# Attention with unnormalised exponentials: reciprocal row sums carried through DRAM to the output projection

## The chip, the cores and the metric

The kernel runs on one core of a Trainium2 chip, in one launch. The metric is the device time of that launch in microseconds (us), the median of several runs. The core has five engines that work through queues of their own: TensorE (PE in the profile, with its weight loads as PEld), VectorE (DVE), ScalarE (ACT), GpSimd (POOL) and SyncE (SP), which in this kernel issues most of the DMA transfers. Each engine takes its instructions strictly in the order of its queue, and waits on semaphores for the others.

## What is computed

One trunk layer over 1280 tokens: 1024 latent tokens and 256 context tokens, D_MODEL = 1024. Everything is float32. Of the layer, this concerns the attention and the projection behind it:

```
def one_block(qi):
    s = jnp.einsum('bqkgd,bskd->bkgqs', qi, kf) * scale
    p = jax.nn.softmax(s, axis=-1)
    return jnp.einsum('bkgqs,bskd->bqkgd', p, vf)
...
o_a = block_attention(q, k_all, v_all)
o_h, s_final = hgrn_branch(...)
g = jax.nn.sigmoid(gl.astype(F32)).reshape(b, l, N_BRANCH, D_MODEL)
merged = g[:, :, 0] * (o_h @ w_ho) + g[:, :, 1] * (o_a @ w_ao)
return merged @ w_out, k, v, s_final
```

There are 8 query heads of 64 channels on 2 key/value heads. A latent token attends to 512 cached keys and all 1024 latent keys; a context token attends to the 256 context keys. `o_h` is the output of a second branch, a gated linear recurrence (the HGRN branch, 4 heads of 128 channels). Behind the mixer stand a residual, a second norm and an MLP of width 4096.

## The kernel before

**Tiles and stages.** The tokens are cut into three token tiles `TT`: t = 0 and t = 1 with 512 latent tokens each, t = 2 with the 256 context tokens. Products in full precision are made of three TensorE products: every operand is split into a rounded high part `hi` (ACT, line 277) and a rest `lo` (DVE, line 278), and `hi*hi`, `hi*lo` and `lo*hi` are added in PSUM (lines 308 to 310 and 325 to 327). The program runs in this order: input norm and the first projections; attention, into which the projections of the HGRN branch are interleaved; the HGRN recurrence, into which the projections of the branch gates GL are interleaved; the output projection of both branches; the rest of the layer with the MLP.

**One unit of attention.** `Unit` (line 661) stands for one head, one token tile and 256 query rows (`q2` counts these within the tile, `j` is 0 or 1 for the two blocks of 128 rows). For t < 2 the keys come in three groups of 512 (`i` = 0, 1, 2), so a unit has six tasks (j, i); for t = 2 there is one group of 256 keys and a unit has two tasks. There are 32 long units and 8 short ones. The steps of a task are:

- `score` (line 686): PE makes the scores in PSUM (`ps_s`, line 697), DVE takes their row maximum (`mx`, line 698) and, when the block's groups are all there, the negated overall maximum (`ngm`, line 702).
- `expo` (line 705): ACT makes the exponentials in SBUF (`pexp`, line 708) and at the same time their row sums (`sm`). After the block's last group DVE adds the sums of the groups (`rs`, line 711) and takes the reciprocal (line 712).
- `norm` (line 714): each tile of exponentials is multiplied with the reciprocal `rs` of its row, in place. `NORM = [g_, v]` hands these products in turn to POOL and to DVE (line 716).
- `trans` (line 733): PE turns 256 keys by 256 queries of the weighted exponentials (`ps_t`, line 738); ACT and DVE split them into `pTh` (line 741) and `pTl` (line 742).
- `value` (line 745): PE multiplies the values `Vl` with `pTh` (line 753) and with `pTl` (line 754), and adds over all keys. At the unit's end ACT and DVE bring the two halves of the result together (`pvt`, line 762, and `oa`, line 763). When the second head of a pair has done its last rows of the token tile, the pair's outputs, 128 channels by n tokens, go to DRAM as `OA` (line 766).

**What sets the order.** `events` (line 718) lists a unit's steps with a place in time each, counted in transposes of 256 keys; `attention` (line 791) sorts the events of all units, and in front of each lets `Filler` issue its share of the interleaved projections. That fixes the order of PE's queue, which is scheduled by hand. The queues of DVE, ACT, POOL and SP are put in order by the framework, from the same program and a model of the durations. Small tiles such as `mx`, `sm` and (after the change) `rs` come from rings: `T(4)` has 8 buffers of 4 columns each, which are used again in turn, each once its last reader is done; where that reader is a DMA, the next writer waits for the DMA.

**The interleaved projections.** Their weights come as `wraw` (1 MB per DMA, two buffers, line 282) and are split by ACT and DVE into `wsp` (128 x 1024 per instruction, lines 277 and 278).

**The output projection.** Lines 1141 to 1149 load, for t in the order 0, 2, 1, the eight tiles of 128 channels by n tokens, four of the HGRN branch (`OH`) and four of attention (`OA`), into tiles `or`, and split each into two `hs` tiles. The `hs` tiles are the buffers in which the normed input `hT` of the layer has stood until then, so a split waits until the last product of the GL projection with that buffer is done. The `or` tiles come from a ring of 20 buffers in SBUF (ring "X"). From line 1165 on PE multiplies them with the two branches' weights, DVE gates the results (line 1182).

Of the kernel before, what the change touches and what calls it, by code (L numbers as in the profile page):

```python
# [12 lines left out]
ALU = mybir.AluOpType  # L13
AX = mybir.AxisListType

P = 128
# [9 lines left out]
TT = [(0, 512, 0), (512, 512, 0), (1024, 256, 1)]  # L26
# [18 lines left out]
def build(ctx, tc, I, O, C):  # L45
    nc = tc.nc
    v, s_, g_, pe, sp = nc.vector, nc.scalar, nc.gpsimd, nc.tensor, nc.sync
# [42 lines left out]
    def H(t, dt=F32R, name="hs"):  # L90

        return hp.tile([P, 512] if t < 2 else [P, 2, 256], dt, tag="h%d" % t, name=name, bufs=16 if t < 2 else 8)

    def T(n, name="tiny"):
        return tp.tile([P, n], F32, tag="tiny%d" % n, name=name, bufs=8 if n <= 16 else 2)

    def DR(shape, name, dt=F32):
        return dp.tile(list(shape), dt, name=name)

    def dma(out, in_):  # L100
        sp.dma_start(out=f32(out), in_=f32(in_))
# [4 lines left out]
    def f32(ap):  # L106
        return ap.bitcast(F32)
# [105 lines left out]
    def hpair(t):  # L213
        n = TT[t][1]
        if n == 512:
            return H(t), H(t)
        x = h_first.pop() if h_first else H(2)
        return x[:, 0, :], x[:, 1, :]
# [57 lines left out]
    def split(hi, lo, raw):  # L276
        s_.activation(hi, raw, AF.Copy)  # L277
        return v.tensor_tensor(lo, raw, f32(hi), op=ALU.subtract)  # L278
# [104 lines left out]
    KG = [512, 512, 512, 256]  # L383
# [205 lines left out]
    for idx in range(len(steps)):  # L589
        while idx >= KC - 1 and done <= min(idx + AHEAD, len(steps) - 1):  # L590
            t, kc = steps[done]
# [7 lines left out]
        t, kc = steps[idx]  # L599
# [58 lines left out]
    OA = [[DR((P, n), "OA%d_%d" % (c, t)) for t, (_, n, _) in enumerate(TT)] for c in range(4)]  # L658
    OH = [[DR((P, n), "OH%d_%d" % (c, t)) for t, (_, n, _) in enumerate(TT)] for c in range(4)]

    class Unit:


# [22 lines left out]
        def score(self, j, i):  # L686
            nk = len(self.kts)
            if (j, i) == (0, 0):
                self.qh = q_at[self.h, self.t]
                self.ps, self.mx, self.sm, self.rs = {}, {}, {}, {}  # L690
            if i == 0:
                self.mx[j], self.sm[j] = T(4, "mx"), T(4, "sm")
            n = KG[self.kts[i]]
            q0 = self.q2 * 256 + j * P
            pq = PS("s")
            for var in range(2):
                pe.matmul(pq[:, 0:n], self.qh[:, q0:q0 + P], K[self.g][var][self.kts[i]], start=(var == 0), stop=(var == 1))  # L697
            v.tensor_reduce(self.mx[j][:, i:i + 1], pq[:, 0:n], axis=AX.X, op=ALU.max)  # L698
            self.ps[j, i] = pq
            if i == nk - 1:  # L700
                ngm = T(1, "ngm")
                v.tensor_reduce(ngm, self.mx[j][:, 0:nk], axis=AX.X, op=ALU.max, negate=True)  # L702
                self.mx[j] = ngm

        def expo(self, j, i):
            n, nk = KG[self.kts[i]], len(self.kts)
            e = self.Ps[j][i] = S(name="pexp")
            s_.activation(e[:, 0:n], self.ps.pop((j, i))[:, 0:n], AF.Exp, bias=self.mx[j], accum_out=self.sm[j][:, i:i + 1])  # L708
            if i == nk - 1:
                rs = self.rs[j] = T(1, "rs")  # L710
                v.tensor_reduce(rs, self.sm[j][:, 0:nk], axis=AX.X, op=ALU.add)
                v.reciprocal(rs, rs)

        def norm(self, j, i):
            x = self.Ps[j][i][:, 0:KG[self.kts[i]]]
            NORM[(i + j) % len(NORM)].tensor_scalar(x, x, self.rs[j], None, op0=ALU.mult)  # L716

        def events(self, s0):
            if self.nstep == 1:
                ev = [(-4, 0, 0), (-3.5, 1, 0)]  # L720
                out = [(a, self.score, (j, i)) for a, j, i in ev]
                out += [(a + 1, self.expo, (j, i)) for a, j, i in ev]
                out += [(a + 2, self.norm, (j, i)) for a, j, i in ev]
            else:
                out = [(a, self.score, (j, i)) for (j, i), a in zip(self.tasks, (-7, -6.9, -6, -4, -3.9, -3))]
                out += [(a, self.expo, (j, i)) for (j, i), a in zip(self.tasks, (-5.4, -4.9, -4.4, -2.4, -1.9, -1.4))]
                out += [(a, self.norm, (j, i)) for (j, i), a in zip(self.tasks, (-4.35, -3.45, -2.45, -1.35, 0.1, 2.1))]
            for p2 in range(self.nstep):
                out.append((p2, self.trans, (p2,)))
                out.append((p2 + ((2.5, 2.3, 2.0, 1.7, 1.5, 1.3)[p2] if self.nstep > 1 else 1.5), self.value, (p2,)))  # L730
            return [(s0 + a, f, x) for a, f, x in out]
# [33 lines left out]
            if self.h % 2 == 1 and self.q2 == n // 256 - 1:  # L765
                dma(OA[self.h // 2][self.t], o_at[self.h // 2, self.t][:, 0:n])

    NORM = [g_, v]
    gone, keyed, copied = [None], [None], [None]
    q_at, o_at = {}, {}  # L770
    K = [[[None] * 4 for _ in range(2)] for _ in range(2)]
    V = [[None] * 4 for _ in range(2)]

# [17 lines left out]
    def attention(fill):  # L791
        units = []
        for ts_ in ((0, 1), (2,)):
            for h0 in (4, 6, 0, 2):
                for t in ts_:
                    for hh in range(2):
                        for q2 in range(TT[t][1] // 256):
                            units.append(Unit(h0 // 4, h0 + hh, t, q2, [0, 1, 2] if t < 2 else [3],
                                              q2 == 0 and (t < 2 or hh == 0), hh == 0 and q2 == 0))
        events, s0 = [], 0  # L800
        for u in units:
            if u.new_q:
# [340 lines left out]
    for t in MT:  # L1143
        n = TT[t][1]
        for c in range(8):
            r = S(name="or")
            dma(r[:, 0:n], (OH if c < 4 else OA)[c % 4][t])
            oT[t][c] = hpair(t)
            split(oT[t][c][0], oT[t][c][1], r[:, 0:n])
    mg = [[None] * KC for _ in range(3)]  # L1150
# [14 lines left out]
    for c2 in range(4):  # L1165
        r = wp.tile([P, 8, 256], F32, tag="wraw", name="wraw", bufs=2)
        for i, nm in enumerate(("w_hgrn_out", "w_attn_out")):
            dma(r[:, 4 * i:4 * i + 4, :], I[nm][:, c2 * 256:(c2 + 1) * 256].rearrange("(k p) c -> p k c", p=P))
        for half in range(2):
# [4 lines left out]
            for t in MT:  # L1174
                n = TT[t][1]
# [108 lines left out]
    for b, half in turns:  # L1284
        t, off = b // 4, (b % 4) * P
# [62 lines left out]
    def raw1(i):  # L1348
        return wraw(I["w_ff1"], KC, i * 256)
# [30 lines left out]
    for i in range(NP):  # L1380
        r = raw1(i)
        for half in range(2):
            j = 2 * i + half
# [5 lines left out]
            if half == 0:  # L1389

                x = pw.tile([P, 4, P], F32, tag="at", name="at", bufs=4)
# [43 lines left out]
    ev = pool("ev", "right")  # L1435
    W2 = I["w_ff2"]
    op0 = []
# [221 lines left out]
    def fw_tile(name):  # L1659
        return xo.tile([P, D], F32, tag="fw", name=name, bufs=1)  # L1660
# [80 lines left out]
    x = fw_tile("y34")  # L1741
# [85 lines left out]
```

## Time and profile before

| | |
|---|---|
| median of 3 runs | 2055.07 us (2054.92 to 2057.83) |
| the profiled execution, its own time | 2055.24 us |
| span of its instructions | 2053.1 us, at a mean granted TensorE clock of 0.998 |
| attention, by the first and last split of transposed exponentials | 171.8 to 706.8 us |
| DVE busy from 153 to 714 us | 394.18 of 561.00 us |
| POOL busy from 153 to 714 us | 181.68 of 561.00 us |
| DMA from 153 to 714 us | 0.24 of the engines' time, 78 GB/s |
| splits of `or` tiles (DVE) | 24, from 1024.4 to 1039.7 us |

The profile names a group of instructions by the line that records it, the engine, the operation and the tiles, as `out<-in`. A time "idle before" is how long the engine had nothing to do just before an instruction; behind `<-` stands what released it. In a timeline each row gives the start, the time that the row's instructions cover, and in brackets the idle time before it. Matmuls are pipelined: the next one starts before the one before it has ended, so that two starts lie closer together than one matmul lasts.

### The profile page before, as it was taken

Reading aid. Unit: us, or ns where it says so; the run is one execution under the profiler, and the core shown is the slowest. Engines: PE = TensorE matmul, PEld = TensorE weight load, DVE = VectorE, ACT = ScalarE, POOL = GpSimd, SP = SyncE. Lnnn points to the kernel's source line nnn. Section 1 sums busy time; section 2 is a strip of 40 time slices with the busy share of each in tenths; the row PEclk is TensorE's granted clock in tenths of the full one; section 3 lists DMA queues with packets and bytes.
Section 4 is the critical chain, followed back from the end, with each engine's and each line's share of the span. In section 5 each row is a group of like instructions: output and inputs, shape, how many; then the busy total and the mean of one; then the engine's idle time right before and its main releaser. Section 6 shows DMA issues by size and latency. Waiting matters only on the chain.

```text
span 2053.1 us, 33691 instructions
## 1 busy us (share of the span) xinstructions
PE 2012.3 (98%) x12470; PEld 1736.1 (85%) x12470; DVE 1405.3 (68%) x2655; ACT 938.5 (46%) x1906; POOL 546.1 (27%) x566
## 2 busy tenths in 40 slices
PE   6899999999999999999999999999999999999998
PEld 5798889988889988888888889998888888888886
DVE  4876776777776788779254634886666666577686
ACT  4735555555555423332321335655455544333443
POOL 1473333333332265545112101222122110000130
PEclk9999999999999999999999999999999999999999
DMA  9453220322211455455544533864444489455764
GB/s 309 150 187 97 78 77 27 108 86 78 78 45 65 132 175 167 153 173 159 196 138 149 180 113 116 259 186 151 157 147 157 145 292 361 148 159 176 232 238 142
DMA packets 220052, 317.38 MB, mean 155 GB/s; under 512 B 18504, under 2 KB 139168, under 8 KB 219888
## 3 DMA queue, kind: packets, MB, share of 16 engines
q1 hardware_dynamic: 207216, 275.05, 41.7%
q0 software_dynamic: 12672, 40.18, 5.5%
q8 instruction: 98, 1.61, 0.3%
q14 instruction: 66, 0.54, 0.1%
HBM read 229.43 MB, written 85.74 MB: 154 GB/s over the span
## 4 chain that ended last, share of the span: by engine, by line
PE 62%; DVE 2%; issue 1%; ACT 0%; DMA 0%; POOL 0%; POOLq 0%; ACTq 0%; DVEq 0%
PE ps_g L308 5%; PE ps_g L309 5%; PE ps_g L310 5%; PE ps_g L1614 2%; PE ps_g L1616 2%; PE ps_g L1615 2%; PE ps_s L1460 2%; PE ps_s L1461 2%; PE ps_s L1459 2%; PE ps_s L1614 2%; PE ps_s L1615 2%; PE ps_s L1616 2%; PE ps_t L1614 2%; PE ps_t L1615 2%; PE ps_t L1616 2%; PE ps_s L308 2%
## 5 line engine op out<-in xcount | busy, mean ns | idle before, releaser
L308 PE MATMUL ps_g<-hs,wsp 128*128 128x512 f32 (+1 forms) x896 | 322.2, 360 | 1.1 <-DVE adas L186 1.0
L310 PE MATMUL ps_g<-hs,wsp 128*128 128x512 f32 (+1 forms) x896 | 309.3, 345 | 0.0
L309 PE MATMUL ps_g<-hs,wsp 128*128 128x512 f32 (+1 forms) x896 | 309.1, 345 | 0.0
L716 POOL TENSOR_SCALAR pexp<-pexp,rs 128x512 f32<-128x512 f32 (+1 forms) x104 | 171.5, 1655 | 364.8 <-ACT pTh L741 210.6
L277 ACT ACTIVATE wsp<-wraw 128x1024 fp32r<-128x1024 f32 x110 | 109.7, 997 | 276.6 <-PE ps_g L309 82.8
L278 DVE TENSOR_TENSOR wsp<-wraw,wsp 128x1024 fp32r<-128x1024 f32 x110 | 139.9, 1272 | 114.8 <-ACT wsp L277 114.4
L308 PEld LDWEIGHTS ps_g<-hs,wsp 128*128 128x128 f32 x896 | 169.6, 189 | 22.3 <-issue 4.6
L310 PEld LDWEIGHTS ps_g<-hs,wsp 128*128 128x128 f32 x896 | 169.3, 189 | 21.5
L309 PEld LDWEIGHTS ps_g<-hs,wsp 128*128 128x128 f32 x896 | 169.9, 190 | 14.8
L741 ACT ACTIVATE pTh<-ps_t 128x512 fp32r<-128x512 f32 x200 | 118.4, 603 | 124.5 <-PE ps_t L738 124.4
L277 ACT ACTIVATE ah<-ar 128x640 fp32r<-128x640 f32 (+1 forms) x112 | 80.9, 723 | 185.1 <-PE ps_g L1615 102.3
L698 DVE TENSOR_REDUCE mx<-ps_s 128x1 f32<-128x512 f32 (+1 forms) x208 | 137.1, 663 | 37.7 <-PE ps_s L697 36.9
L708 ACT ACTIVATE pexp<-ps_s,ngm 128x512 f32<-128x512 f32 (+1 forms) x208 | 137.4, 670 | 43.7 <-DVE ngm L702 42.9
L278 DVE TENSOR_TENSOR ah<-ar,ah 128x640 fp32r<-128x640 f32 (+1 forms) x112 | 93.1, 832 | 77.2 <-ACT ah L277 76.1
L742 DVE TENSOR_TENSOR pTl<-ps_t,pTh 128x512 fp32r<-128x512 f32 x200 | 135.9, 681 | 14.1 <-ACT pTh L741 13.9
L697 PE MATMUL ps_s<-Kl,Ql 128*128 128x512 f32 (+1 forms) x416 | 130.7, 411 | 0.7 <-ACT pexp L708 0.7
L738 PE MATMUL ps_t<-ident,pexp 128*128 128x128 f32 x800 | 120.8, 273 | 3.3 <-DVE pTl L742 1.8
L325 PE MATMUL ps_g<-wsp,hs 128*128 128x256 f32 x400 | 115.9, 290 | 0.0
L327 PE MATMUL ps_g<-wsp,hs 128*128 128x256 f32 x400 | 112.9, 282 | 0.0
L326 PE MATMUL ps_g<-wsp,hs 128*128 128x256 f32 x400 | 112.5, 281 | 0.0
L754 PE MATMUL ps_g<-pTl,Vl 128*128 128x256 f32 x400 | 105.9, 287 | 4.0 <-DVE pTl L742 4.0
L738 PEld LDWEIGHTS ps_t<-ident,pexp 128*128 128x128 f32 x800 | 93.6, 140 | 14.1 <-issue 4.0
(421 smaller groups left out, 5395.2 us busy)
## 6 DMA issues: line engine op xcount, KB each, us to landing
ar<-AF SPq DMA_DIRECT2D x112, 320.0 KB, 3.2
wraw<-in_w_ff SPq DMA_DIRECT2D x32, 1024.0 KB, 6.1
wr<-in_w_ff SPq DMA_DIRECT2D x128, 256.0 KB, 4.4
wraw<-in_w_in SPq DMA_DIRECT2D x18, 1024.0 KB, 5.7
wraw<-in_w_ada SPq DMA_DIRECT2D x16, 1024.0 KB, 5.6
AF<-a POOLq DMA_DIRECT2D x48, 256.0 KB, 2.7
AF<-t POOLq DMA_DIRECT2D x48, 256.0 KB, 2.4
wa<-in_w_ada SPq DMA_DIRECT2D x32, 256.0 KB, 5.8
```

Source lines behind the costliest of these rows:

```text
L277: s_.activation(hi, raw, AF.Copy)
L278: return v.tensor_tensor(lo, raw, f32(hi), op=ALU.subtract)
L308: pe.matmul(out, hi[:, k, :], mh, start=(first and k == 0), stop=False)
L309: pe.matmul(out, hi[:, k, :], ml, start=False, stop=False)
L310: pe.matmul(out, lo[:, k, :], mh, start=False, stop=(last and k == kcs - 1))
L697: pe.matmul(pq[:, 0:n], self.qh[:, q0:q0 + P], K[self.g][var][self.kts[i]], start=(var == 0), stop=(var == 1))
L698: v.tensor_reduce(self.mx[j][:, i:i + 1], pq[:, 0:n], axis=AX.X, op=ALU.max)
L708: s_.activation(e[:, 0:n], self.ps.pop((j, i))[:, 0:n], AF.Exp, bias=self.mx[j], accum_out=self.sm[j][:, i:i + 1])
L716: NORM[(i + j) % len(NORM)].tensor_scalar(x, x, self.rs[j], None, op0=ALU.mult)
L738: pe.transpose(pt[:, a, j * P:(j + 1) * P], self.Ps[j][i][:, b * P:(b + 1) * P], ident)
L742: v.tensor_tensor(lo, pt, f32(hi), op=ALU.subtract)
L1614: pe.matmul(bank, ph, wh, start=first and i == 0, stop=False, **more)
```

## The change

The step `norm` is gone. The exponentials go unnormalised into `trans` and `value`, so `OA` holds sums that are not yet divided. The reciprocals of a head and token tile are gathered in one small tile `rs` of four columns (two for t = 2), one for each block of 128 rows. After the last block, DVE takes one reciprocal of all columns, and SP writes them to a new DRAM tensor `RS` of n floats, in the order of the tokens: column c of the tile goes to elements 128c to 128c + 127, so neighbouring elements of the destination come from different partitions. That makes 24 small stores, one for each of 8 heads and 3 token tiles.

In the output projection each of the 12 loads of an `OA` tile is followed by two loads of reciprocals: the `RS` row of the first head of the pair is broadcast to partitions 0 to 63 of a second `or` tile, that of the second head to partitions 64 to 127. DVE multiplies the `OA` tile with it, in place, and the tile is then split as before.

```
-                self.ps, self.mx, self.sm, self.rs = {}, {}, {}, {}
+                self.ps, self.mx, self.sm = {}, {}, {}
...
             if i == nk - 1:
-                rs = self.rs[j] = T(1, "rs")
-                v.tensor_reduce(rs, self.sm[j][:, 0:nk], axis=AX.X, op=ALU.add)
-                v.reciprocal(rs, rs)
-
-        def norm(self, j, i):
-            x = self.Ps[j][i][:, 0:KG[self.kts[i]]]
-            NORM[(i + j) % len(NORM)].tensor_scalar(x, x, self.rs[j], None, op0=ALU.mult)
+                col, n = 2 * self.q2 + j, TT[self.t][1] // P
+                if col == 0:
+                    rs_at[self.h, self.t] = T(4, "rs")
+                rs = rs_at[self.h, self.t]
+                v.tensor_reduce(rs[:, col:col + 1], self.sm[j][:, 0:nk], axis=AX.X, op=ALU.add)
+                if col == n - 1:
+                    v.reciprocal(rs[:, 0:n], rs[:, 0:n])
+                    dma(RS[self.h][self.t].rearrange("(c p) -> p c", p=P), rs[:, 0:n])
...
-                out += [(a + 2, self.norm, (j, i)) for a, j, i in ev]
...
-                out += [(a, self.norm, (j, i)) for (j, i), a in zip(self.tasks, (-4.35, -3.45, -2.45, -1.35, 0.1, 2.1))]
...
             dma(r[:, 0:n], (OH if c < 4 else OA)[c % 4][t])
+            if c >= 4:
+                q = S(name="or")
+                for i in range(2):
+                    dma(q[64 * i:64 * i + 64, 0:n], RS[2 * (c - 4) + i][t].unsqueeze(0).broadcast_to([64, n]))
+                v.tensor_tensor(r[:, 0:n], r[:, 0:n], q[:, 0:n], op=ALU.mult)
```

PE's queue is the same in both kernels, instruction for instruction. ACT's differs in a few neighbours that have changed places. POOL's has lost its 104 products and nothing else.

DVE's queue during attention, at about 576 to 582 us of the profile before, where the row sums of a block of head 3 and t = 0 are formed. `pTl` is the split of the transposed exponentials, `mx` and `ngm` belong to the row maxima, `rs` to the row sums. Before:

```order
L742 TENSOR_TENSOR pTl<-ps_t,pTh 128x512
L702 TENSOR_REDUCE ngm<-mx 128x1
L711 TENSOR_REDUCE rs<-sm 128x1
L712 RECIPROCAL rs<-rs 128x1
L716 TENSOR_SCALAR pexp<-pexp,rs 128x512 x2
L742 TENSOR_TENSOR pTl<-ps_t,pTh 128x512
L698 TENSOR_REDUCE mx<-ps_s 128x1
```

And now, around the same split:

```order
L743 TENSOR_TENSOR pTl<-ps_t,pTh 128x512
L704 TENSOR_REDUCE ngm<-mx 128x1
L716 TENSOR_REDUCE rs<-sm 128x1
L743 TENSOR_TENSOR pTl<-ps_t,pTh 128x512
L700 TENSOR_REDUCE mx<-ps_s 128x1
L743 TENSOR_TENSOR pTl<-ps_t,pTh 128x512
```

Three instructions between the sum of the row sums and the split behind it are gone; the sum itself keeps its place.

DVE's queue in front of the output projection, from the last but one split of GL weights (`wsp`) on, or from the last: `hs<-or` are the splits, `or<-or` in the changed kernel the products with the reciprocals, `gt` the gating of the first results. Before:

```order
L278 TENSOR_TENSOR wsp<-wraw,wsp 128x1024 x2
L278 TENSOR_TENSOR hs<-or,hs 128x512 x15
L278 TENSOR_TENSOR hs<-or,hs 128x256 x3
L278 TENSOR_TENSOR hs<-or,hs 128x512
L278 TENSOR_TENSOR hs<-or,hs 128x256 x4
L278 TENSOR_TENSOR wsp<-wraw,wsp 128x1024
L1182 SCALAR_TENSOR_TENSOR gt_13048<-gt_13048,ps_s 128x512
L278 TENSOR_TENSOR hs<-or,hs 128x256
```

And now, from the products of the 256-token tile on:

```order
L1152 TENSOR_TENSOR or<-or 128x256 x4
L278 TENSOR_TENSOR wsp<-wraw,wsp 128x1024
L278 TENSOR_TENSOR hs<-or,hs 128x512 x9
L1152 TENSOR_TENSOR or<-or 128x512
L278 TENSOR_TENSOR hs<-or,hs 128x512 x4
L1152 TENSOR_TENSOR or<-or 128x512
L278 TENSOR_TENSOR hs<-or,hs 128x256
L1152 TENSOR_TENSOR or<-or 128x512
L278 TENSOR_TENSOR hs<-or,hs 128x256 x3
L278 TENSOR_TENSOR hs<-or,hs 128x512
L1152 TENSOR_TENSOR or<-or 128x512
L278 TENSOR_TENSOR hs<-or,hs 128x256 x3
```

The products for t = 0 and t = 2 stand ahead of all splits; the four for t = 1 stand among them, and splits for t = 1 and t = 2 stand behind each.

More of the change, by code (lines that the diff above doesn't have):

```diff
@@ L659, in build @@
     OH = [[DR((P, n), "OH%d_%d" % (c, t)) for t, (_, n, _) in enumerate(TT)] for c in range(4)]
+    RS = [[DR((n,), "RS%d_%d" % (h, t)) for t, (_, n, _) in enumerate(TT)] for h in range(8)]
     class Unit:
@@ L766, in value @@
                 dma(OA[self.h // 2][self.t], o_at[self.h // 2, self.t][:, 0:n])
-    NORM = [g_, v]
     gone, keyed, copied = [None], [None], [None]
-    q_at, o_at = {}, {}
+    q_at, o_at, rs_at = {}, {}, {}
     K = [[[None] * 4 for _ in range(2)] for _ in range(2)]
```

## The prediction

> **What bounds the kernel now.** I read the page's busy times first, then the busy time by stage, then PE's waits inside attention, then the timelines around single waits. The page's head and its first part, with busy us, share of the span and count for each engine:
>
> ```profile
> span 2053.1 us, 33691 instructions
> PE 2012.3 (98%) x12470; PEld 1736.1 (85%) x12470; DVE 1405.3 (68%) x2655; ACT 938.5 (46%) x1906; POOL 546.1 (27%) x566
> ```
>
> PE is busy almost throughout, so a gain can only come from the little that PE waits. The same by stage; the columns are the stage, its length, then PE, PEld, DVE, ACT and POOL, each with its busy us and count, then clock and DMA:
>
> ```profile
> 153.00:714.00 561.00, 553.05 (x3999) 500.16 (x3997) 394.18 (x866) 313.25 (x737) 181.68 (x112) 1.00 0.24 78
> 1000.00:1275.00 275.00, 274.65 (x1417) 234.81 (x1416) 126.98 (x199) 85.64 (x161) 38.10 (x37) 1.00 0.44 145
> ```
>
> The first row is attention: PE lacks 8.0 us, DVE is used to 70%. The second holds the output projection: PE lacks 0.35 us. The clock is full in both. PE's waits inside attention, in the answer on waits (engine, tile and line waited for, us in total, times, longest):
>
> ```profile
> PE ps_g L754 <- DVE pTl L742: 4.0, 10, 0.8
> PE ps_t L738 <- DVE pTl L742: 1.8, 3, 0.9
> PE ps_t L738 <- DVE pexp L716: 1.3, 3, 0.7
> PE ps_s L697 <- ACT pexp L708: 0.7, 2, 0.4
> ```
>
> That is 7.8 us in 18 waits. All but two name DVE, though DVE is idle for 30% of the stage: it is late in places. One wait shows what it really costs, on PE:
>
> ```profile
> 580.40 0.28 PE L753 MATMUL ps_g<-pTh,Vl 128*128 128x256 f32 x1
> 581.05 0.39 PE L754 MATMUL ps_g<-pTl,Vl 128*128 128x256 f32 x1 [0.37 <-DVE pTl L742]
> 581.27 0.27 PE L753 MATMUL ps_g<-pTh,Vl 128*128 128x256 f32 x1
> 581.39 0.28 PE L754 MATMUL ps_g<-pTl,Vl 128*128 128x256 f32 x1
> ```
>
> Undisturbed, these products start 0.12 us apart (581.27 to 581.39). Here it was 0.65, so 0.53 us were lost where the trace counts 0.37 of idle time: 0.16 more for each wait, because the pipeline runs empty. The 18 waits therefore cost about 7.8 + 18 x 0.16 = 10.7 us, and that is the most that attention can give.
>
> **Part 1: the products go.** What DVE did in front of that wait:
>
> ```profile
> 578.69 0.16 DVE L711 TENSOR_REDUCE rs<-sm 128x1 f32<-128x3 f32 x1 [2.19 <-ACT pexp L708]
> 578.88 0.17 DVE L712 RECIPROCAL rs<-rs 128x1 f32<-128x1 f32 x1
> 579.08 1.32 DVE L716 TENSOR_SCALAR pexp<-pexp,rs 128x512 f32<-128x512 f32 x2
> 580.32 0.68 DVE L742 TENSOR_TENSOR pTl<-ps_t,pTh 128x512 fp32r<-128x512 f32 x1
> ```
>
> DVE stands for 2.19 us at the row sums, which come from ACT's last exponential, then does a reciprocal and two products, and only then the split that PE needs. From the end of the sum to the split it is about 1.5 us, of which the products take 1.24 (579.08 to 580.32). In the changed queue the split follows the sum directly, so it ends about 1.4 us earlier and the 0.53 us wait is gone. In the whole stage this is what is removed:
>
> ```profile
> L716 POOL TENSOR_SCALAR pexp<-pexp,rs x104: 925/1760/2350, 164.1 to 696.3; 128x512 f32<-128x512 f32 x96, 128x256 f32<-128x256 f32 x8
> L716 DVE TENSOR_SCALAR pexp<-pexp,rs x104: 333/487/1124, 164.7 to 697.5; 128x512 f32<-128x512 f32 x96, 128x256 f32<-128x256 f32 x8
> L712 DVE RECIPROCAL rs<-rs x80: 144/164/167, 163.8 to 696.8; 128x1 f32<-128x1 f32 x80
> ```
>
> On DVE 104 products of 0.487 us by the median make at least 51 us, and 56 of 80 reciprocals of 0.16 us make 9 us: 60 of 394 us. POOL's 104 products of 1.76 us, 183 us, are worth nothing by themselves, since just 3 of the 18 waits (1.3 us) name a product at all.
>
> Which waits go? The 10 waits of L754 and the 3 that name `pexp`: in the timeline most of them have one or two products directly in front of the late split. They cost 5.3 + 13 x 0.16 = 7.4 us. One of these will stay, because nothing of the change stands in front of it:
>
> ```profile
> 374.62 1.23 DVE L278 TENSOR_TENSOR wsp<-wraw,wsp 128x1024 fp32r<-128x1024 f32 x1 [0.52 <-ACT wsp L277]
> 375.77 0.69 DVE L698 TENSOR_REDUCE mx<-ps_s 128x1 f32<-128x512 f32 x1
> 376.37 0.68 DVE L742 TENSOR_TENSOR pTl<-ps_t,pTh 128x512 fp32r<-128x512 f32 x1
> 377.11 0.39 PE L754 MATMUL ps_g<-pTl,Vl 128*128 128x256 f32 x1 [0.57 <-DVE pTl L742]
> ```
>
> DVE was idle for 0.52 us in front of the weight split, so products further ahead cost it nothing; the 1.23 us weight split and a maximum made the wait (0.57 + 0.16 = 0.73). That leaves 7.4 - 0.7 = 6.7 us of gain. The other 5 waits (1.8 + 0.7 + 5 x 0.16 = 3.3 us) stay in the forecast.
>
> What is late next is the weight split and the sum itself, which DVE still awaits:
>
> ```profile
> DVE rs L711 <- ACT pexp L708: 89.1, 49, 2.6
> ```
>
> A split placed behind such a sum has 1.8 us less (89.1/49) than the queue's work suggests. Some of the 1.24 us saved will be spent waiting at one of these, as at 374.62. I take 1.0 us back for that; the bounds are nothing and all of the 6.7.
>
> **Part 2: the stores of the reciprocals.** 24 of them join SP's queue. Each waits for DVE's reciprocal; queued behind it are stores of `ze` tiles, loads of queries and of `wraw`. ACT already waits for the latter:
>
> ```profile
> ACT wsp L277 <- DMA wraw<-in_w_in: 13.1, 9, 2.8
> OA<-oa SPq DMA_DIRECT2D x8, 256.0 KB, 2.3
> q1 hardware_dynamic: 207216, 275.05, 41.7%
> ```
>
> The nearest store lands in 2.3 us at 256 KB; these hold 2 KB, but as 512 single floats. By the last row (packets, MB, share of 16 engines' span) a packet took on average 0.417 x 16 x 2053.1 us / 207216 = 66 ns. So 512 pieces would take, by estimate, 2.1 us on 16 engines and 34 us on one. Their readers are far off: the next user of the buffer comes about one unit later, and a unit is 6 of the 199 steps between these times, (706.8 - 171.8) / 199 x 6 = 16 us:
>
> ```profile
> L742 DVE TENSOR_TENSOR pTl<-ps_t,pTh x200: 671/681/694, 171.8 to 706.8; 128x512 fp32r<-128x512 f32 x100
> ```
>
> I take 0 for the stores, with the rows near 2 us; the bounds are 0 and 1.5 us (nine `wraw` loads, each late by 0.16 us, the length of the sum in front of the reciprocal). The Trainium skill speaks against this store: DMA: Bandwidth & Descriptors, section Rules for kernel authors, says that a non-contiguous last dimension is lowered to one descriptor per element and should be rearranged. No run here shows such a DMA. By that rule the sum would have the 512 pieces that I counted, and stay as it is while the engines share them.
>
> **Part 3: the output projection.** DVE gets 12 products, SP 24 loads. Eight products stand ahead of the splits, in the gap of 12.55 us below. The four for t = 1 do not:
>
> ```profile
> 1023.25 1.22 DVE L278 TENSOR_TENSOR wsp<-wraw,wsp 128x1024 fp32r<-128x1024 f32 x1 [12.55 <-ACT wsp L277]
> 1024.39 3.70 DVE L278 TENSOR_TENSOR hs<-or,hs 128x512 fp32r<-128x512 f32 x6
> 1028.94 5.00 DVE L278 TENSOR_TENSOR hs<-or,hs 128x512 fp32r<-128x512 f32 x8 [0.85 <-ACT hs L277]
> 1039.74 0.42 DVE L278 TENSOR_TENSOR hs<-or,hs 128x256 fp32r<-128x256 f32 x1
> 1025.53 0.93 SPq L101 DMA_DIRECT2D or<-OA  x2
> or<-OA SPq DMA_DIRECT2D x8, 256.0 KB, 6.5
> 1043.83 0.28 PE L308 MATMUL ps_g<-hs,wsp 128*128 128x256 f32 x1
> ```
>
> The last split for t = 2 ends at 1040.2; PE uses it at 1043.8 (the last of four steps, t = 2, attention half). The slack is 3.6 us. Four products of 0.62 us (as the splits, 5.00/8) take 2.5. The first of them stands behind the ninth split, at about 1030.2, but its `OA` tile, loaded at 1025.5, lands 6.5 us later, at 1032.0: 1.8 us of waiting. Together 4.3 us against 3.6 of slack: a wait of 0.7 us, of which DVE's idle 0.85 us can take a part. I take 0.3; the bounds are 0 and 2 us (the loads late by another 1.3, as SP now issues three for each tile). Later stages see the same queues.
>
> **The sum.** -6.7 + 1.0 + 0 + 0.3 = -5.4 us. PE's queue is the same and PE is full behind attention, so what it gains there arrives at the end. From the profiled execution's own 2055.24 us (2.1 more than its span, and 0.2 more than the median of the runs) that gives **2049.8 us**. The bounds are 2055.24 - 10.7 = 2044.5 and, with 6.7 taken back, 1.5 and 2 added, 2058.7.
>
> **The rivals.**
> - *The waits are refilled.* The sums that hold DVE for 1.8 us and the weight splits of 1.23 us take over. For it: the 89.1 us above stand and DVE was never full. Against it: the change at 578.69 leaves nothing between sum and split. It gives back 3.5 to 6.7 us: 2052 to 2055.
> - *All waits go*, also the 3.3 us that I left, since some of those splits have moved ahead of a maximum: 2055.2 - 10 = 2045.5. Against it: the wait at 377.11.
> - *The store becomes the wait.* If the 512 pieces land through one engine in 34 us, the ACT or DVE instruction that uses the `rs` buffer next waits for it. It decides at 16 us of landing time; every us above that costs one for each of the 16 long stores: at 20 us 16 x 4 - 5 = 59 us lost, 2114, and more beyond. Against it: the nearest stores land in 2.3 us. The Trainium skill's rule on single elements, named above, is what this rival would look like at its worst.
>
> **How the numbers follow.** Chances: forecast 0.62 (2046.5 to 2052), refilled 0.24, all waits go 0.08, the store 0.06. The range of 2045.5 to 2053.5 leaves out the store and the weaker half of "refilled". A measurement can tell 0.2%, 4.1 us: faster is below 2051.0. That holds most of the forecast (0.56) and all of the second rival: 0.64. The same: the rest of the forecast and most of "refilled", 0.28. Slower: the store and a tail of parts 2 and 3, 0.08.
>
> **What would show it.** Right: PE's idle time from 153 to 714 us falls from 8.0 to about 3 us, the waits L754 on `pTl` to one or two, and the rest name `pTl` behind a weight split or a maximum. DVE's busy time in the stage falls to about 335 us. PE's idle time from 1000 to 1275 us stays below 1.5 us. A store of reciprocals lands in 2 to 4 us. Wrong: as many waits on `pTl` as before; DVE or ACT released by a DMA from `rs`; PE waiting for `hs` around 1044 us.

## The result: slower by 1.4%

| | before | after |
|---|---|---|
| median of the runs, us | 2055.29 (2054.92 to 2057.83) | 2084.8 (2081.3 to 2088.87) |
| the profiled execution, us | 2055.24 | 2086.68 |

The ratio after to before is 1.0141, 95% interval 1.0128 to 1.0154: 29.5 us slower. The prediction said 5.4 us faster, and its range ended at 2053.5.

PE's queue is the same in both kernels, so the n-th product of one can be set against the n-th of the other. The table has how much later (+) such a product starts than its twin before, in the profiled executions; the last column is the last product of all. From one column to the next is what the stretch between them costs.

| product that started before at, us | 172.9 | 631.7 | 717.6 | 971.0 | 1051.2 | 2044.8 |
|---|---|---|---|---|---|---|
| after | +1.4 | -4.9 | +27.4 | +25.5 | +30.3 | +31.4 |

From 172.9 to 631.7 lie the long units of attention (t = 0 and 1): 6.3 us won. From 631.7 to 717.6 lie the eight short units (t = 2), where no loss was forecast: 32.3 us lost. The output projection (971.0 to 1051.2) loses 4.8 instead of 0.3. The rest is within 2 us.

The profile after, first the page's head and its first part, and then the time by stage in the columns of the prediction:

```profile
span 2084.6 us, 33371 instructions
PE 2021.6 (97%) x12470; PEld 1746.8 (84%) x12470; DVE 1349.1 (65%) x2507; ACT 939.0 (45%) x1906; POOL 373.4 (18%) x462
```

```profile
153.00:714.00 561.00, 539.74 (x3848) 489.19 (x3848) 324.70 (x691) 308.01 (x725) 6.45 (x5) 0.98 0.26 76
1000.00:1275.00 275.00, 271.90 (x1402) 230.19 (x1401) 128.07 (x219) 78.04 (x162) 40.40 (x41) 0.99 0.49 157
620.00:740.00 120.00, 96.28 (x735) 93.06 (x732) 50.34 (x133) 46.92 (x115) 3.88 (x3) 0.89 0.39 70
```

The last row again, of the kernel before:

```profile
620.00:740.00 120.00, 117.56 (x1027) 111.00 (x1025) 87.14 (x213) 54.91 (x130) 42.62 (x34) 1.00 0.35 113
```

DVE and POOL have less to do, as intended. But between 620 and 740 us PE lacks 23.7 us where it lacked 2.4, and its granted clock (third number from the end) is 0.89 instead of 1.00. Both count. Between the two products of the table (626.8 to 745.0 us after, 631.7 to 717.6 before) PE idles 22.8 us longer, and the same 723 products keep it busy 9.5 us longer. Together that is the 32 us. PE's waits after, as in the prediction, those at the kernel's start left out:

```profile
...
PE ps_s L699 <- ACT pexp L710: 7.4, 2, 6.9
PE ps_g L754 <- DVE oa L764: 6.8, 1, 6.8
...
PE ps_t L739 <- DVE adas L186: 3.9, 1, 3.9
PE ps_s L699 <- DMA Kl<-KS: 3.7, 1, 3.7
PE ps_g L309 <- DVE hs L278: 2.8, 2, 2.0
PE ps_t L739 <- DVE pTl L743: 2.4, 3, 1.3
...
PE ps_g L755 <- DVE pTl L743: 1.7, 3, 1.0
```

The waits on `pTl` (rows `L739` and `L755`) have fallen from 5.8 to 4.1 us. Above them stand four single waits of 3.7 to 6.9 us, each with another name, all new, all between 629 and 736 us; the row `hs` is the projection. One of the four in the timeline (rows of several engines):

```profile
695.26 0.39 SPq L101 DMA_DIRECT2D wraw<-in_w_in  x1
...
696.96 8.28 SPq L101 DMA_DIRECT2D RS<-rs  x1
...
699.10 0.28 PE L327 MATMUL ps_g<-wsp,hs 128*128 128x256 f32 x1
699.22 0.28 PE L325 MATMUL ps_g<-wsp,hs 128*128 128x256 f32 x1
...
701.13 0.15 DVE L716 TENSOR_REDUCE rs<-sm 128x1 f32<-128x1 f32 x1 [4.36 <-DMA RS<-rs]
...
707.77 1.06 ACT L277 ACTIVATE wsp<-wraw 128x1024 fp32r<-128x1024 f32 x1 [8.88 <-DMA wraw<-in_w_in]
...
709.34 0.80 PE L699 MATMUL ps_s<-Kl,Ql 128*128 128x256 f32 x2 [6.89 <-ACT pexp L710]
...
709.93 0.41 PE L325 MATMUL ps_g<-wsp,hs 128*128 128x256 f32 x1
...
710.15 0.41 PE L326 MATMUL ps_g<-wsp,hs 128*128 128x256 f32 x1
```

Two things run late here, and both are a DMA. DVE's row sum stands 4.36 us because its `rs` buffer is still being stored. ACT stands 8.88 us for weights that were asked for at 695.26 and landed 12.5 us later; behind it on ACT stands the exponential that frees PE's score buffer. SP itself sat 8.28 us in the issue of one store. And after such a stop PE's products follow each other in 0.22 us (709.93, 710.15) instead of 0.12 (699.10, 699.22): from 706 to 712 us the granted clock is 0.50, and such stretches of 3.4 to 6.8 us, around and after PE's stops, make the mean of 0.89. The stores themselves, in the answer on transfers for 180 to 610 us (first row) and for 610 to 735 us (number, size, median us from issue to landing):

```profile
RS<-rs SPq DMA_DIRECT2D x14, 2.0 KB, 8.9
RS<-rs SPq DMA_DIRECT2D x8, 1.0 KB, 14.5
RS<-rs SPq DMA_DIRECT2D x2, 2.0 KB, 8.7
```

The prediction took 2 us.

### The profile page after: what moved, and what is told of

It reads as the page before. It is cut to its first block, busy times and chain, and to the rows that moved or that the text cites. A ratio compares the mean times of both kernels' runs of the same rounds, so it can differ in the third digit from the quotient of the medians.

```text
span 2084.6 us, 33371 instructions
## 1 busy us (share of the span) xinstructions
PE 2021.6 (97%) x12470; PEld 1746.8 (84%) x12470; DVE 1349.1 (65%) x2507; ACT 939.0 (45%) x1906; POOL 373.4 (18%) x462
## 4 chain that ended last, share of the span: by engine, by line
PE 83%; DMA 6%; DVE 4%; ACT 1%; issue 1%; POOL 1%; SPq 0%; POOLq 0%; DVEq 0%; ACTq 0%
PE ps_g L308 8%; PE ps_g L309 7%; PE ps_g L310 7%; PE ps_s L699 4%; PE ps_t L739 4%; DMA wraw<-in_w_in 2%; PE ps_g L1621 2%; PE ps_g L1620 2%; PE ps_g L1619 2%; PE ps_s L1464 2%; PE ps_s L1465 2%; PE ps_s L1466 2%; PE ps_g L755 2%; PE ps_g L754 2%; PE ps_s L310 2%; PE ps_s L309 2%
## 5 line engine op out<-in xcount | busy, mean ns | idle before, releaser
L739 PE MATMUL ps_t<-ident,pexp 128*128 128x128 f32 x800 | 121.0, 274 | 6.3 <-DVE adas L186 3.9
L325 PE MATMUL ps_g<-wsp,hs 128*128 128x256 f32 x400 | 118.2, 296 | 0.0
L861 POOL TENSOR_TENSOR ze<-ze,hnb 128x512 f32<-128x512 f32 x10 | 13.8, 1382 | 580.2 <-DVE ze L859 569.7
L327 PE MATMUL ps_g<-wsp,hs 128*128 128x256 f32 x400 | 115.1, 288 | 0.0
L326 PE MATMUL ps_g<-wsp,hs 128*128 128x256 f32 x400 | 114.7, 287 | 0.0
L754 PE MATMUL ps_g<-pTh,Vl 128*128 128x256 f32 x400 | 105.4, 285 | 8.7 <-DVE oa L764 6.8
L739 PEld LDWEIGHTS ps_t<-ident,pexp 128*128 128x128 f32 x800 | 94.4, 141 | 16.2 <-issue 8.2
```

Of the source, the lines that this page charges most:

```text
L739: pe.transpose(pt[:, a, j * P:(j + 1) * P], self.Ps[j][i][:, b * P:(b + 1) * P], ident)
L754: pe.matmul(pv[:, 0:256], V[self.g][kg][:, b, :], hi[:, a, :], start=(k == 0), stop=False)
```

## Experiments

Unless it says otherwise, each run is the changed kernel with one edit. The table has the medians, the ratio to the kernel before with its interval (before ran beside each at 2054.4 to 2056.0), and what three stretches cost against their twins before (the long units, the short units and the projection), and how late the last product starts. The time is the median of several runs, the stretches are those of the one profiled execution. Up to the first product of the long units the runs stand at -0.1 to +2.8.

| run | us | ratio, 95% interval | long | short | projection | last |
|---|---|---|---|---|---|---|
| the change | 2084.8 | 1.0128 to 1.0154 | -6.3 | +32.3 | +4.8 | +31.4 |
| e1 own buffers | 2075.7 | 1.0088 to 1.0137 | -7.1 | +25.8 | +1.9 | +20.4 |
| e2 POOL's queue | 2069.1 | 1.0052 to 1.0082 | -8.8 | +17.1 | +4.6 | +13.6 |
| e3 fewer pieces | 2054.3 | 0.9988 to 1.0008 | -9.1 | +4.0 | +1.6 | -2.7 |
| e4 no store | 2051.9 | 0.9972 to 0.9991 | -8.8 | -0.2 | +5.4 | -2.8 |
| e5 stores alone | 2081.5 | 1.0116 to 1.0144 | -3.8 | +30.0 | 0.0 | +28.6 |
| e6 no scaling | 2074.5 | 1.0078 to 1.0105 | -7.9 | +29.2 | 0.0 | +19.6 |
| e7 one store, paired loads | 2089.9 | 1.0156 to 1.0184 | -9.1 | -0.3 | +43.2 | +34.9 |
| e8 the same, own ring | 2075.2 | 1.0086 to 1.0114 | -8.9 | -0.2 | +28.6 | +18.3 |
| e9 one store | 2051.3 | 0.9966 to 0.9984 | -8.8 | +0.1 | +4.7 | -3.4 |
| e10 one store, own ring | 2047.3 | 0.9946 to 0.9971 | -8.4 | +0.1 | +0.7 | -6.9 |
| e11 POOL's queue, own buffers | 2068.8 | 1.0048 to 1.0075 | -8.6 | +18.3 | +4.6 | +15.2 |
| e12 pieces 512 bytes apart | 2052.3 | 0.9975 to 0.9994 | -9.1 | -0.4 | +4.1 | -4.4 |
| e13 pieces 64 bytes apart | 2050.3 | 0.9966 to 0.9985 | -8.8 | +0.1 | +4.4 | -0.8 |
| e14 pieces 16 bytes apart | 2053.5 | 0.9978 to 0.9997 | -7.9 | +0.3 | +6.7 | -0.9 |

### Whose wait is it: the buffer's, or the queue's? (e1, e2, e11)

The trace shows both, so each was taken away alone, and then both. e1 gives every `rs` tile columns of its own in a tile that is free by then:

```
-                    rs_at[self.h, self.t] = T(4, "rs")
+                    k = 3 * self.h + self.t
+                    rs_at[self.h, self.t] = qk[:, 4 * k:4 * k + 4]
```

> Each of the 24 rs tiles gets columns of its own (the query and key norm weights' tile, which is no longer read by then), so no maximum, row sum or exponential waits for a store before its buffer is used again; the stores stay on SP's queue. Theory Q (the queue: the 512 or 256 single floats of a store hold up everything that stands behind them on SP's queue): the loads of weights and keys and the stores of oa still land late, PE still stands at the weight split near 630 us, at the keys near 681, at the row behind the weights near 702 and at oa near 729; those four are 21.8 of the 22 us, so 2076 to 2085 us. Theory B (the buffers: ACT and DVE wait for the store that still reads the rs buffer): the waits of ACT and DVE on RS go, and with them most of the loss: 2055 to 2062 us.

It measured 2075.7 us, just below the range of theory Q: 9 us come back, 6.5 of them in the short units. Theory Q holds for the larger part. The late loads and stores are still there (ACT's and DVE's waits, 600 to 760 us; `wsp` is line 278 here and `oa` line 766):

```profile
ACT wsp L278 <- DMA wraw<-in_w_in: 24.0, 3, 11.2
...
DVE oa L766 <- DMA OA<-oa: 8.1, 1, 8.1
```

e2 sends the stores through POOL's queue:

```
-                    dma(RS[self.h][self.t].rearrange("(c p) -> p c", p=P), rs[:, 0:n])
+                    store(RS[self.h][self.t].rearrange("(c p) -> p c", p=P), rs[:, 0:n])
```

> The 24 stores are issued by POOL instead of SP, from the same ring of eight buffers. Theory Q: SP's loads and stores land as in the kernel before and the four stalls of PE go; what is left is the cost of the output projection (about 5 us) against a gain of about 6 in attention: 2052 to 2058 us, if the rs buffers do not hold by themselves. Theory B: the stores land as late as before, buffers come free as late, 2075 to 2085 us.

2069.1 us lies between the two expectations: half the loss of the short units is gone (17.1 of 32.3 left). Theory Q as I had put it is not enough, and ACT still waited 5.4 us for a store to free its buffer. So e11 makes both edits:

> The stores in single floats stay, but both of their followers go: they are issued by POOL and their tiles have columns of their own. If what stands behind them on SP and the buffers that they hold are all the ways in which they cost, attention and the projection are as without stores: 2051 to 2056 us. If the pieces also slow the other transfers on the way to memory, 2058 to 2068 us.

2068.8 us, as e2. With none of SP's transfers queued behind a store and no buffer held by one, 18.3 of the 32.3 us that the short units lose stay. The second expectation, a third way, holds, though the time lies just above its range. The transfers of 600 to 735 us in e11:

```profile
wraw<-in_w_in SPq DMA_DIRECT2D x2, 1024.0 KB, 10.8
VD<-ze SPq DMA_DIRECT2D x5, 256.0 KB, 6.4
OA<-oa SPq DMA_DIRECT2D x4, 128.0 KB, 14.1
RS<-qk POOLq DMA_DIRECT2D x8, 1.0 KB, 13.6
```

The same of e10, which has no such store there:

```profile
wraw<-in_w_in SPq DMA_DIRECT2D x3, 1024.0 KB, 5.7
VD<-ze SPq DMA_DIRECT2D x5, 256.0 KB, 2.2
OA<-oa SPq DMA_DIRECT2D x4, 128.0 KB, 2.6
```

These medians rest on the few transfers whose landing the trace has. The clearest pair is in e11 itself: the `VD` store that went at 636.32, with no such store under way, landed in 2.7 us, the one at 682.14, beside several, in 10.0; so transfers of another queue land late while a store in single floats is under way. The Trainium skill (DMA: Bandwidth & Descriptors, section Queues, rings and completion order) says that the count which reports a transfer's end is written only after every earlier write of the same DMA engine, across its queues. The trace fits this, with `VD` at 10.0 instead of 2.7 us, but the count is not all. The data is late too. What SP's queue moved from 600 to 735 us (packets, MB, share of the 16 engines' time), in e11 and then in e10:

```profile
q1 hardware_dynamic: 9274, 10.38, 37.2%
```

```profile
q1 hardware_dynamic: 13388, 14.65, 33.2%
```

In e11 the engines spent more time on less data. Between 610 and 745 us, 43 of its packets of 512 to 4096 bytes took over 2 us each, where the median packet takes 46 ns; e10 and e12 have none.

### What makes the store slow? (e3, e4, e5)

e3 stores the same bytes in another order, so that each partition's floats lie together in DRAM:

```
-                    dma(RS[self.h][self.t].rearrange("(c p) -> p c", p=P), rs[:, 0:n])
+                    dma(RS[self.h][self.t].rearrange("(p c) -> p c", p=P), rs[:, 0:n])
```

> The same store of the same bytes from the same tile and queue, but each partition's two or four floats lie side by side in DRAM: 128 pieces of 8 or 16 bytes instead of 256 or 512 of 4. The values reach the projection in another order, so the scaling is of the wrong queries. If the number of pieces sets the landing (9 us for 512, so some 18 ns each), a store lands in 2 to 5 us and the kernel takes 2054 to 2066 us. If it is the store as such (24 more of them on the queue, whatever their pieces), nothing changes: 2080 to 2087 us.

2054.3 us: that one word takes away 30 us. The stores of 128 pieces land in 2.0 us in the long units and 5.4 in the short ones:

```profile
RS<-rs SPq DMA_DIRECT2D x14, 2.0 KB, 2.0
RS<-rs SPq DMA_DIRECT2D x8, 1.0 KB, 5.4
```

It fits the number of pieces, but does not prove it: the pieces are also longer. e4 leaves out the line of the store, and the loads of the projection read rows of `w_in` in place of `RS`:

> No store of row sums at all; the 24 broadcast loads of the output projection read rows of the input weights instead, so the outputs are scaled by other numbers. If the stores are the whole loss in attention, attention keeps its gain of about 6 us and the projection its cost of about 5: 2052 to 2057 us. If the new order on DVE and ACT is to blame in the short units, 2070 to 2085 us.

2051.9 us, within 0.1 us of the first expectation. Without stores the short units lose nothing, and what the change costs in the projection (5.4) stands alone. The order of DVE and ACT is not to blame. e5 goes the other way: the kernel before, with its products, and only the stores added, with a copy of each reciprocal into the tile that is stored:

```
                 v.reciprocal(rs, rs)
+                col, n = 2 * self.q2 + j, TT[self.t][1] // P
+                if col == 0:
+                    rs_at[self.h, self.t] = T(4, "rs")
+                v.tensor_copy(out=rs_at[self.h, self.t][:, col:col + 1], in_=rs)
+                if col == n - 1:
+                    dma(RS[self.h][self.t].rearrange("(c p) -> p c", p=P), rs_at[self.h, self.t][:, 0:n])
```

> The kernel before with nothing taken out: the exponentials are still normalised and the projection is as it was. Only the 24 stores of reciprocals are added, from SP, in single floats, with a copy of each reciprocal into a tile of four columns. If the stores alone make the loss, whatever else the change moves: 2055 + 25 to 35 us (the 26 us lost in attention in the changed kernel, and no gain of 6 to pay a part), 2078 to 2092 us. If the loss needs the changed order of DVE and ACT in the short units: 2055 to 2062 us.

2081.5 us, 27 above its own before: the stores make the loss, without the rest of the change.

### Number, or neighbourhood? (e12, e13, e14)

The Trainium skill's rule that I had weighed (DMA: Bandwidth & Descriptors, section Rules for kernel authors: one descriptor for each element) says something about the number of pieces. e12 keeps the number, the tile, the queue and the line, and puts each float 512 bytes from the last; the loads read `w_in` as in e4.

```
-    RS = [[DR((n,), "RS%d_%d" % (h, t)) for t, (_, n, _) in enumerate(TT)] for h in range(8)]
+    RS = [[DR((n, 128), "RS%d_%d" % (h, t)) for t, (_, n, _) in enumerate(TT)] for h in range(8)]
...
-                    dma(RS[self.h][self.t].rearrange("(c p) -> p c", p=P), rs[:, 0:n])
+                    dma(RS[self.h][self.t].rearrange("(c p) e -> p c e", p=P)[:, :, 0:1], rs[:, 0:n].unsqueeze(2))
```

> The stores in single floats again, from the same tiles on SP, but each float goes 512 bytes from the last instead of beside it; the projection's loads read rows of the input weights (as in the run without stores), so the outputs are scaled by other numbers. Compare with 2084.8 us (floats side by side) and 2051.9 (no stores). If a piece costs what it costs wherever it goes, a long store still lands in about 9 us and the time is 2070 to 2090 us. If neighbouring floats written by different DMA engines hold each other up, a long store lands in 2 to 4 us and the time is 2051 to 2058 us.

2052.3 us: the loss is gone. The page of after counts these packets, and the page of e12 the same ones, with 154 and 156 GB/s:

```profile
DMA packets 232594, 320.03 MB, mean 154 GB/s; under 512 B 29512, under 2 KB 150688, under 8 KB 232432
```

```profile
DMA packets 232594, 320.03 MB, mean 156 GB/s; under 512 B 29512, under 2 KB 150688, under 8 KB 232432
```

And e12's stores, in the long units and in the short ones:

```profile
RS<-rs SPq DMA_DIRECT2D x14, 2.0 KB, 2.1
RS<-rs SPq DMA_DIRECT2D x8, 1.0 KB, 2.6
```

Packet for packet the same traffic lands in 2.1 us instead of 8.9. So neither the number nor the size of the pieces costs here, but that they are neighbours in DRAM. My reading of e3 by the number of pieces falls with it; that its pieces start 16 bytes apart (8 in the short units) fits better, but no run took that apart from their number and length. How near is near? e13 and e14 are e12 with `(n, 16)` and `(n, 4)` in place of `(n, 128)`:

> As the run with the floats 512 bytes apart, but 64 bytes apart (again without scaling by the stored numbers). The landing of a long store is what tells. If only pieces in the same 64 bytes hold each other up: 2 to 3 us, and 2050 to 2054 us. If the region is longer (512 bytes hold eight floats here): 3 to 6 us of landing and 2052 to 2065 us.

> The same, 16 bytes apart, so four floats share 64 bytes instead of sixteen. If the delay grows with the floats that share 64 bytes: 3 to 5 us of landing, 2053 to 2065 us. If it comes from neighbouring floats in one short word (16 or 32 bytes): 2 to 3 us, 2050 to 2054 us. If any sharing costs the full delay: about 9 us and 2075 to 2087 us.

2050.3 and 2053.5 us. The long stores land in 2.4 us at 64 bytes, 3.0 at 16, 8.9 at 4 bytes. Taken store by store, 64 bytes do not differ from 512 (the first three: 1.8, 1.9 and 1.8 us against 1.8, 2.0 and 1.8), 16 bytes cost a little (2.4, 2.7 and 2.4), and 4 bytes nearly all of it (9.3, 8.8 and 9.0). The first expectation of e13 holds; e14 lies on the border between its first two, so whether the delay grows with the pieces in 64 bytes or begins in a shorter stretch stays open. 3 us are too short for anything in attention to wait (the short units lose 0.3), so it is the landing, not the time, that tells these two apart. Which step of the way to memory makes writes beside each other wait is not shown by any run; in the trace it comes after the packets have been sent. A store's 528 packets of 4 bytes took 7 to 9 ns each and all began within 0.4 us in both kernels; the last completion came 0.5 us after them in e12 (246.86 to 247.34) and 7.7 us after them in the change (247.13 to 254.81).

### What does the projection cost? (e6 to e10)

e6 leaves out the loads and products of the projection, so nothing is divided by the row sums:

```
-            if c >= 4:
-                q = S(name="or")
-                for i in range(2):
-                    dma(q[64 * i:64 * i + 64, 0:n], RS[2 * (c - 4) + i][t].unsqueeze(0).broadcast_to([64, n]))
-                v.tensor_tensor(r[:, 0:n], r[:, 0:n], q[:, 0:n], op=ALU.mult)
```

> The changed kernel with its stores, but the 24 loads and 12 products of the output projection are left out, so the attention outputs stay unnormalised. If the projection costs what its shift shows (5 us between 979 and 1051 us), 2078 to 2081 us; if that shift is only the late wake of the stores, 2084 to 2087 us.

Its projection costs 0.0 instead of 4.8. The time, 2074.5, is lower than expected since the other stretches came out some 5 us better as well, without a reason that I can name; runs with the slow stores scatter by several us (the change itself from 2081.3 to 2088.87).

e7 is what e1 to e5 suggest: all 80 columns of row sums stay in SBUF, and after attention one transposition turns them for a single store in rows of 512 bytes. I also joined the two loads of a broadcast tile:

```
+    v.reciprocal(rs_all, rs_all)
+    rpt = PS("t")
+    pe.transpose(rpt[0:80, 0:P], rs_all, ident)
+    rse = S((80, P), name="ev")
+    s_.activation(rse, rpt[0:80, 0:P], AF.Copy)
+    dma(RSA, rse)
...
-                for i in range(2):
-                    dma(q[64 * i:64 * i + 64, 0:n], RS[2 * (c - 4) + i][t].unsqueeze(0).broadcast_to([64, n]))
+                dma(q[:, 0:n], rs_rows(t)[2 * (c - 4):2 * (c - 4) + 2].unsqueeze(1).broadcast_to([2, 64, n]))
```

> All 80 columns of row sums stay in one tile; after attention there is one reciprocal, one transposition on PE, one copy and one store of 80 rows of 512 bytes. The projection loads one tile for a head pair with one transfer instead of two; all else as in the change. If the single floats are the whole loss and the projection costs 5 us through its waiting for loads: attention 8 to 9 us ahead, projection 3 to 5 behind, 2048 to 2052 us. If the number of loads (12 instead of 24) is what costs there: 2045 to 2048 us. If single floats are not the loss: above 2060 us.

The time lies where the third expectation put it, but the stretches tell otherwise: attention behaves as the first had it (-9.1, -0.3), and the projection loses 43.2 us. DVE, in the timeline:

```profile
1054.04 0.69 DVE L1157 TENSOR_TENSOR or<-or 128x512 f32<-128x512 f32 x1 [7.18 <-DMA or<-RSA]
...
1060.11 0.69 DVE L1157 TENSOR_TENSOR or<-or 128x512 f32<-128x512 f32 x1 [4.17 <-DMA or<-RSA]
...
1066.64 0.69 DVE L1157 TENSOR_TENSOR or<-or 128x512 f32<-128x512 f32 x1 [4.30 <-DMA or<-RSA]
...
1072.72 0.69 DVE L1157 TENSOR_TENSOR or<-or 128x512 f32<-128x512 f32 x1 [3.78 <-DMA or<-RSA]
```

A joined load lands every 6 us. The trace's completions show why: of the 16 that one load gives, 14 came at about 1000.6 us and the last 2 at 1008.3 to 1008.8. The Trainium skill (DMA: Bandwidth & Descriptors, section Rules for kernel authors) says that a transfer whose outermost dimension has c < 16 entries runs on at most c DMA engines. The trace agrees: mine has 2, and 2 completions were late. I had overlooked it. e8 only moves the broadcast tiles to rings of their own:

```
-                q = S(name="or")
+                q = S(name="gt%d" % (c % 2))
```

> As the run with one store, but the broadcast tiles of the projection come from two rings of three buffers that nothing else uses at that time, instead of the ring of 20 that the or tiles share (24 or tiles and 12 broadcast tiles ask for 36 buffers of it). If the loads for t = 1 are late because their buffers come free late, the waits at the projection go: 2045 to 2048 us. If the length of SP's queue or the 12 products set them: as the run with one store, within 1 us.

2075.2 us says little, since the slow transfer hides the rest; that it starts earlier (966 instead of 992 us) gives 15 us back. e9 and e10 are e7 and e8 with two loads for a tile, as in the change:

> One store of row sums after attention, as in the last two runs but one; the projection loads each head's half of a broadcast tile by a transfer of its own, as the change does, into the ring of 20. Attention stays 8 to 9 us ahead. If the 35 and 18 us that those two runs lost at the projection come from the paired transfer (two of its sixteen parts landed 5 to 6 us after the other fourteen), the projection loses what it loses in the changed kernel, 5 us: 2049 to 2053 us. If they come from reading one tensor that is written late, 2070 to 2090 us.

> The same, with the broadcast tiles in the two rings of three buffers. If the late buffers of the shared ring are what makes the loads for t = 1 late, the projection costs under 1.5 us: 2045 to 2048 us. If it is the 24 loads on SP's queue and the 12 products, as with the shared ring: 2049 to 2053 us.

2051.3 and 2047.3 us, both as the first expectation: the joined load was e7's whole loss, and the shared ring makes what the projection costs in e9. With it, 24 `or` and 12 broadcast tiles ask 36 times for 20 buffers, so that loads for t = 1 are issued as late as 1028.38 us; with rings of their own the last three go from 1010.43 on:

```profile
1028.38 1.08 SPq L101 DMA_DIRECT2D or<-RSA  x2
```

```profile
1010.43 2.36 SPq L101 DMA_DIRECT2D gt<-RSA  x3
```

The size of the projection's cost is less sure than its cause: with the same loads and products as in the change, if from other rows in some (e1 to e4, e11 to e14), it is 1.6 to 6.7 us, and why it varies was not tested.

e10 beats both kernels: ratio to before 0.9959, interval 0.9946 to 0.9971. Its attention and its projection:

```profile
153.00:714.00 561.00, 557.75 (x4070) 508.54 (x4069) 338.35 (x697) 315.84 (x742) 14.59 (x12) 1.00 0.25 81
1000.00:1275.00 275.00, 274.15 (x1433) 235.09 (x1432) 135.25 (x214) 89.78 (x167) 39.66 (x39) 1.00 0.46 153
```

PE lacks 3.2 us in attention and 0.85 in the projection, and DVE is busy for 338 us: the numbers that the prediction gave for the change (3, below 1.5, 335) are those of this kernel.

## Why the prediction was wrong

- **What bounds the kernel, and the products: right, a little low.** The forecast for attention was -5.7 (-6.7 and 1.0 taken back). The long units alone gave 6.3 with the slow stores beside them and 7.9 to 9.1 in the runs without them. The truth lies between the forecast and the rival "all waits go" (10 us), nearer to the rival. The 1.0 us taken back was not needed; three places in the long units where PE lost 2.2 us together against before (near 351, 422 and 564 us) do not lose it in e4, so that goes with the stores too. "The waits are refilled" did not happen.
- **Part 2 is the step that failed.** It took a landing of about 2 us and put the stores at 0, with 1.5 as the bound. Side by side the pieces landed in 8.9 us, since they are neighbours and not since they are many: e12 has as many, and they landed in 2.1. That the working by pieces (512 of 66 ns on 16 engines, 2.1 us) gives the same 2.1 us is luck: the 66 ns are the mean of packets of every size, those of these stores took 7 to 9 ns and all began within 0.4 us, so their number makes little of the landing. No row of the trace before had neighbouring 4-byte writes, and the bound from the other side, 34 us on one engine, I had set aside for the row with 256 KB, which was not the nearest in kind. Measured in place of 0: 32.3 us in the short units; the whole kernel is 32.9 us slower than e4, which has no stores.
- **The readers were misjudged too.** That the next user of a buffer comes about one unit later, 16 us, holds for the long units. A short unit is one step of 2.7 us (16/6), so its buffers come round within a landing. And a store that lands in 9 us does harm without any reader: it holds up what is queued behind it on SP (e2 against the change: 15 us of the short units) and slows what runs on other queues (e11: 18 us). I had listed SP's queue behind the stores, but priced only the 0.16 us by which they are issued later.
- **The rival "the store becomes the wait"** named the right place with a chance of 0.06 and the wrong price. It let the loss begin at 16 us of landing time in the long stores; at 8.9 us it had begun in the short ones. The rule of one descriptor for each element, which I had set beside it from the Trainium skill, counts the pieces rightly (512 of them, the packets agree) and does not explain the time: e12 has as many.
- **Part 3 was too small:** 4.8 us for 0.3, above its bound of 2. DVE's 12 products and the slack were worked out, but not the buffers: the broadcast tiles share a ring with the tiles that they scale. With rings of their own, 0.7 (e10).
- **The signs to look for** worked: DVE and ACT released by a DMA from `rs`, and PE waiting for `hs`, at 1069 and 1073 us.

## What to carry to other kernels

Price a small DMA by how its pieces lie in memory, not only by its bytes or their number: before adding one, look for a transfer of the same kind in a trace, and if there is none, keep the slow bound in the range. Collect what is scattered by partition, transpose it once and store it in long rows, and see that the outermost dimension of a broadcast load is not a small one (2 entries cost some 38 us here, 64 did not). A new tile in an old ring takes buffers from its neighbours, so count the requests of a ring before and after a change.

## What the runs showed of the hardware that was not expected

- Stores of 512 floats from 128 partitions landed in 2.1 us with the floats 512 bytes apart in DRAM, 2.4 at 64, 3.0 at 16, and 8.9 side by side. In the trace the 4-byte packets of one such store all began within 0.4 us (246.75 to 247.13), and its completions came 6 to 8 us later (253.18 to 254.81); with the floats 512 bytes apart they came within 0.9 us.
- Such a store delays transfers of another issuing queue: in e11 a store of 256 KB landed in 10.0 us instead of 2.7, and single packets of 1 to 2 KB took up to 6.2 us, where the median is 46 ns.
- SP sat up to 8.28 us in the issue of one of these stores; the median is 0.38 us. Why was not tested.
- Around and after PE's waits the granted clock stood at 0.50 for 3.4 to 6.8 us at a time (0.89 over 120 us), and equal products started 0.22 us apart instead of 0.12; 9.5 of the 32 us lost in the short units are of this kind.
- A broadcast load with an outermost dimension of 2 landed every 6 us; with the same bytes in two loads of 64 partitions, from rings of their own (e10), the whole projection lost 0.7 us.
